# A hybrid encoder layer on one Trainium2 core: exponentials one tick behind their maxima, more gate buffers, gates spread up to the projections, softmax sums inverted behind their transpose

## The chip, the cores and the metric

One core of one Trainium2 chip runs the whole program as a single launch. Its engines run side by side, each in its own program order, and wait for one another by semaphores: TensorE (PE, matmuls and transposes; PEld is its weight load), VectorE (DVE), ScalarE (ACT), GpSimd (POOL) and SyncE (SP), which here only issues DMA transfers, all of them from one queue in program order. The metric is the device time of one execution in microseconds (us); lower is better.

## The reference

One layer on `x` of 1024 tokens by 1024 channels, float32. A first RMS norm and one combined projection give the inputs of two mixers and of two merge gates:

```python
proj = rmsnorm(x, attn_norm_g) @ w_in          # 1024 x 8096
c_q, c_kv, k_rope, z_mla, q_dil, k_dil, v_dil, z_dil, g_mla, g_dil = split(proj)
a_out = mla_attention(c_q, c_kv, k_rope, ...)  # 8 heads, dense softmax over 1024 keys
y_mla = (a_out * silu(z_mla)) @ w_o_mla
d_out = dilated_mixture(q_dil, k_dil, v_dil)   # 3 groups of 8 heads, windows of
...                                            # dilation 1, 4, 16, merged by their sums
y_dil = (d_out * silu(z_dil)) @ w_o_dil
merged = sigmoid(g_mla + b) * y_mla + sigmoid(g_dil + b) * y_dil
return rmsnorm(x + merged @ w_out, final_norm_g)
```

## The kernel before

Every float32 product is made of three matmuls (`mm3`, L142 to L146: high by high, high by low, low by high parts), so that each operand is first split in two: a cast on ACT (L150) and a subtraction on DVE or POOL (L151). A group of three matmuls of 512 columns is called a **step** here.

The program has five stretches. Up to about 220 us it makes latents, rotary tables and the dilated values; up to about 545 us the dilated queries and keys (`blocks`). Then comes **dilated attention** (to about 832 us), then **latent attention** (to about 1120 us), and last the projections and the output.

*Dilated attention* (`attention`, L1316) is software-pipelined over 72 units: four head pairs, each with 8 units of group 0, 8 of group 1 (`dil_head`, four units a head) and 2 of group 2 (`dil_classes`). The loop L1330 runs ticks t = -2 to 73. In tick t it transposes the probabilities of unit t on PE and copies them out on ACT (`do(t, 3)`, L1144 and L1152), scores unit t+2 on PE (L1120, L1121, or L1231), takes the low part of unit t's transposed probabilities on DVE (L1156), takes the maxima of unit t+2 on DVE (L1130), and later in the same tick the exponentials of unit t+2 on ACT (`do(t + 2, 2)`, L1137); values of unit t-1 follow on PE (L1168, L1175). When the last unit of a head or class group has been scored, the operands of the item after next are loaded into the buffers that this frees (L1339).

Between these the tick *feeds* PE twice with steps of other work (`feed`, L66, a credit counter): `DIL_FEED[g]` steps each time, where g is the group of unit t: 1.33 for groups 0 and 1, 2.3 for group 2. The work fed is `gate_fill` (L718): 16 weight tiles (8 of the z gates, then 8 of the merge gates) by two halves are 32 jobs of 8 steps, 256 steps in all. A job ends in a tail: DVE multiplies the bank by the tokens' factors into a gate buffer `zg_z` (L728), ACT makes a tanh (L730 or L734), POOL two products for z gates (L731, L732), and SP stores the result. Gate buffers are `zg_z` and `zg_t`, two each, in the 128x2048 tile `zt`. The next weight tile is loaded (`w_raw`) at a job's first step and split four steps on.

*Latent attention* (`mla_attention`, L1008) runs 128 ticks: 32 units k (a head and 256 queries) by 4 ticks c. Each tick transposes a quarter of unit k's probabilities (L871), copies them on ACT (L873), takes their low part on DVE (L879), and multiplies by the values of a tick before (L895, L896). Scores, maxima (L855) and exponentials (L863, their sums go to `m_den`) of unit k+1 run in ticks c = 0 to 2. Ticks c = 2 and 3 feed PE with `self.rate` steps. Gates that are left are spread over the ticks before `GATES_END` = 29; nothing is fed from then to `PROJ_BEGIN` = 33, where the dilated projection (`proj_fill`) takes over.

After the second head of a pair, each half of the tokens ends with a division by the softmax sums, eight times in all, at k = 5, 7, 13, 15, 21, 23, 27, 31. `mla_factors` (L917) doubles and inverts the sums on DVE as 128x8 in the last tick of the unit before; `mla_spread` (L929) transposes the result on PE to 8x128 (L938), copies it on ACT (L940), and SP sends it through DRAM (`s_mr`) to all partitions; `mla_gated` multiplies it by the gate on POOL (L953), `mla_weighted` applies it on DVE (L960), and `mla_merged` splits the result (L967). In tick 0 of a unit DVE's order is: low part, then the maxima of the next unit.

The order on each engine in both attention stretches is the order in which the code is written (a manual schedule).

## Time and profile before

| | us |
|---|---|
| median of the runs (two of the three at 1252.39 and 1254.29; one, 4276.14, is far off) | 1254.29 |
| the profiled execution's own time | 1254.46 |
| its span, first to last instruction | 1252.5 |
| TensorE busy in the span | 1212.4 (97%) |
| VectorE, ScalarE, GpSimd busy | 730.8, 622.0, 570.2 |
| mean granted TensorE clock | 0.990 |
| DMA share of the 16 engines, whole span | 59.5% |

All durations below come from that one execution. A busy TensorE is not TensorE at its peak: matmuls overlap, so that a matmul of 0.39 us can start 0.23 us after the one before it. What the engine can lose is its idle time, and stretches in which its granted clock is under 1. On the page, "<-" behind an idle time names what ended it.

### The profile page before, as it was taken

How to read it: one execution, taken by the hardware profiler on the slowest of the kernel's cores; microseconds unless marked ns; L12 is line 12 of the kernel's file. 1: busy time of each engine (PE TensorE's matmuls, PEld its weight loads, DVE VectorE, ACT ScalarE, POOL GpSimd, SP SyncE). 2: the span in 40 equal slices, each digit the busy share in tenths (PEclk: the TensorE clock that was granted, in tenths of full speed). 3: DMA queues.
4: the chain of work that ended last, by engine and by line, in shares of the span. 5: the costliest groups of instructions: out<-in, count | busy, mean ns of one | idle time of the engine just before them, and what ended most of it. 6: DMA issues, size and time to landing. Idle time of an engine off the chain costs nothing.

```text
span 1252.5 us, 19486 instructions
## 1 busy us (share of the span) xinstructions
PE 1212.4 (97%) x6909; PEld 1064.5 (85%) x6909; DVE 730.8 (58%) x1304; ACT 622.0 (50%) x1300; POOL 570.2 (46%) x482
## 2 busy tenths in 40 slices
PE   8979999999999999999999999999999999999998
PEld 8979999888888888888888889878878888888886
DVE  7473534467657653345555575647766767759542
ACT  6534345444343344455554666545655656654232
POOL 2352218877777777543464442415521201168322
PEclk9989999999999999999999999899999999999999
DMA  9847589365445642496887898964634445225241
GB/s 333 225 157 283 196 302 317 103 180 156 135 132 165 174 127 100 122 268 197 233 257 200 207 294 212 266 175 116 178 128 119 110 118 135 85 96 182 84 151 51
DMA packets 126416, 221.37 MB, mean 177 GB/s; under 512 B 28072, under 2 KB 60400, under 8 KB 121392
## 3 DMA queue, kind: packets, MB, share of 16 engines
q1 hardware_dynamic: 126320, 220.14, 59.5%
q8 instruction: 54, 0.88, 0.3%
q14 instruction: 42, 0.34, 0.1%
HBM read 149.24 MB, written 70.85 MB: 176 GB/s over the span
## 4 chain that ended last, share of the span: by engine, by line
PE 75%; DMA 11%; DVE 4%; ACT 4%; issue 3%; POOL 1%; SPq 1%; ACTq 0%; POOLq 0%; DVEq 0%
PE bank L145 5%; PE bank L144 5%; PE bank L146 5%; PE pj L145 4%; PE bank L871 4%; PE pj L144 4%; PE pj L146 4%; DMA at_r<-s_dk 3%; PE st_a L144 2%; PE st_a L145 2%; PE st_d L145 2%; PE st_c L145 2%; PE st_d L146 2%; PE st_a L146 2%; PE st_c L146 2%
## 5 line engine op out<-in xcount | busy, mean ns | idle before, releaser
L151 POOL TENSOR_TENSOR w_l<-w_raw,w_h 128x512 fp32r<-128x512 f32 x188 | 247.5, 1330 | 276.7 <-ACT w_h L150 218.1
L150 ACT CAST w_h<-w_raw 128x512 fp32r<-128x512 f32 x188 | 112.6, 621 | 110.1 <-POOL w_raw L495 92.7
L144 PE MATMUL bank<-at_r,w_h 128*128 128x512 f32 x344 | 142.8, 415 | 0.0
L879 DVE TENSOR_TENSOR at_r<-bank,at_r 128x512 fp32r<-128x512 f32 x128 | 88.0, 688 | 84.5 <-ACT at_r L873 84.2
L145 PE MATMUL bank<-at_r,w_h 128*128 128x512 f32 x344 | 136.6, 397 | 0.6 <-POOL at_r L151 0.6
L146 PE MATMUL bank<-at_r,w_l 128*128 128x512 f32 x344 | 136.7, 397 | 0.0
L873 ACT CAST at_r<-bank 128x512 fp32r<-128x512 f32 x128 | 74.9, 586 | 72.5 <-PE bank L871 71.9
L145 PE MATMUL pj<-w_l,at_r 128*128 128x256 f32 x384 | 109.7, 286 | 0.0
L146 PE MATMUL pj<-w_h,at_r 128*128 128x256 f32 x384 | 109.6, 285 | 0.0
L144 PE MATMUL pj<-w_h,at_r 128*128 128x256 f32 x384 | 109.5, 285 | 0.0
L1137 ACT ACTIVATE at_f<-at_f,at_f 128x256 f32<-128x256 f32 x128 | 64.1, 502 | 52.1 <-DVE at_f L1130 51.8
L1156 DVE TENSOR_TENSOR at_r<-bank,at_r 128x512 fp32r<-128x512 f32 x64 | 43.9, 686 | 70.4 <-ACT at_r L1152 70.3
L495 POOL TENSOR_TENSOR w_raw<-w_raw 128x512 f32<-128x512 f32 x64 | 82.8, 1294 | 0.1
L871 PE MATMUL bank<-consts,at_f 128*128 128x128 f32 x512 | 77.2, 273 | 1.7 <-ACT at_f L863 1.1
L146 PEld LDWEIGHTS bank<-at_r,w_l 128*128 128x128 f32 x344 | 65.7, 191 | 14.9
L146 PEld LDWEIGHTS pj<-w_h,at_r 128*128 128x128 f32 x384 | 74.2, 193 | 1.0
L145 PEld LDWEIGHTS pj<-w_l,at_r 128*128 128x128 f32 x384 | 74.3, 193 | 0.7
L144 PEld LDWEIGHTS pj<-w_h,at_r 128*128 128x128 f32 x384 | 74.2, 193 | 0.7
L145 PEld LDWEIGHTS bank<-at_r,w_h 128*128 128x128 f32 x344 | 65.9, 192 | 9.9 <-POOL at_r L151 1.0
L144 PEld LDWEIGHTS bank<-at_r,w_h 128*128 128x128 f32 x344 | 65.8, 191 | 9.2
L895 PE MATMUL bank<-at_r,at_r 128*128 128x256 f32 x256 | 67.7, 285 | 1.3 <-ACT at_r L873 1.3
L896 PE MATMUL bank<-at_r,at_r 128*128 128x256 f32 x256 | 67.5, 285 | 0.9 <-DVE at_r L879 0.9
(321 smaller groups left out, 3325.3 us busy)
## 6 DMA issues: line engine op xcount, KB each, us to landing
w_raw<-wt SPq DMA_DIRECT2D x48, 512.0 KB, 3.7
at_r<-s_dq SPq DMA_DIRECT2D x32, 512.0 KB, 7.3
s_dk<-dq_st SPq DMA_DIRECT2D x80, 128.0 KB, 2.4
s_dv<-dv_st SPq DMA_DIRECT2D x32, 256.0 KB, 3.0
s_dq<-dq_st SPq DMA_DIRECT2D x64, 128.0 KB, 2.4
zt<-s_gt SPq DMA_DIRECT2D x32, 256.0 KB, 4.5
w_raw<-wv SPq DMA_DIRECT2D x12, 512.0 KB, 5.8
at_r<-s_dk SPq DMA_DIRECT2D x8, 576.0 KB, 11.3
```

The costliest lines, as they stand in the source:

```text
L144: mm(out, lh, rh, start=start, stop=False, skip_group_check=skip)
L145: mm(out, lh, rl, start=False, stop=False, skip_group_check=skip)
L146: return mm(out, ll, rh, start=False, stop=stop, skip_group_check=skip)
L150: self.nc.scalar.copy(out=h, in_=raw)
L151: sub.tensor_tensor(out=l, in0=raw, in1=h.bitcast(F32), op=ALU.subtract)
L495: self.nc.gpsimd.tensor_tensor(out=b[out], in0=b[x], in1=b[y], op=ALU.subtract)
L871: self.nc.tensor.transpose(pt[:, o:o + 128], self.P[k, b][:, 128 * kc:128 * kc + 128], self.ident)
L873: self.nc.scalar.copy(out=h, in_=pt)
L879: self.nc.vector.tensor_tensor(out=l, in0=pt, in1=h.bitcast(F32), op=ALU.subtract)
L895: mm(out, vv[:, kc], ph[:, x], start=kc == 0, stop=False)
L896: mm(out, vv[:, kc], pl[:, x], start=False, stop=kc == 7)
L1137: nc.scalar.activation(out=p, in_=p, func=AF.Exp, scale=-1.0, bias=nm, accum_out=den)
```

## The change

- **Exponentials** of unit t+1, not t+2, run in tick t, and stand directly behind the maxima of unit t+2 and ahead of the feeds. So they come a tick after their maxima, and in the tick ahead of their transposes.
- **Feed**: 1.26 steps in place of 1.33 for groups 0 and 1, and the group is that of unit t+2, the one whose scores are made, not of unit t. At the end of dilated attention steps are fed up to 224 of 256, and the credit is cleared.
- **Gate buffers**: `zg_t` gets two more places, in the unused ends of the key buffers of the dilated heads; jobs 16 to 25 have four places (`zg_g`, all of `zt`) in place of two.
- **Gates to the projections**: `GATES_END` is 33, so that the 32 steps left are 2 in each of the 16 ticks before it that feed. The tokens' factors `R` stay in use longer; one operand of the dilated projection (`brd`, its last) is therefore cut in halves of which one lies where the masks were, and the masks get a fixed address. The two merges at k = 5 and 7 move one unit later, since their place is still read by the gates.
- **Softmax sums**: `mla_factors` is gone. `mla_spread` transposes the sums themselves, and DVE doubles and inverts them from PSUM as 8x128, ahead of the next maxima. ACT's copy is gone.

```diff
-DIL_FEED = (1.33, 1.33, 2.3, 1.8)
+DIL_FEED = (1.26, 1.26, 2.3, 1.8)
+WIDE_END = 26
-GATES_END, PROJ_BEGIN = 29, 33
+GATES_END = PROJ_BEGIN = 33
...
-        for name, k in (("zg_z", 0), ("zg_t", 2), ("br_x", 2), ("gate", 0)):
-            self.places[name] = [right[:, 512 * (k + i):512 * (k + i) + 512] for i in range(4 if name == "gate" else 2)]
+        x = [right[:, 512 * i:512 * i + 512] for i in range(4)]
+        self.places.update(zg_z=x[:2], zg_t=x[2:] + [22528, 30720], zg_g=x, br_x=x[2:], gate=x)
...
-            z = self.get("zg_z")
+            z = self.get("zg_g" if 16 <= job < WIDE_END else "zg_z")
...
-    def mla_factors(self, k):
...
-        d = self.md = self.ep.tile([128, 2, 4], F32, name="m_d", bufs=2)
-        v.tensor_scalar(out=d, in0=self.stats[pair][1][:, :, 4 * half:4 * half + 4], scalar1=2.0, scalar2=None, op0=ALU.mult)
-        v.reciprocal(out=d, in_=d)
...
-        nc.tensor.transpose(tp[:8, :128], d.rearrange("p h b -> p (h b)"), self.ident)
+        nc.tensor.transpose(tp[:8, :128], self.stats[pair][1][:, half].rearrange("p h b -> p (h b)"), self.ident)
         ds = self.get("av_t")[:8, :128]
-        nc.scalar.copy(out=ds, in_=tp[:8, :128])
+        nc.vector.tensor_scalar(out=ds, in0=tp[:8, :128], scalar1=2.0, scalar2=None, op0=ALU.mult)
+        nc.vector.reciprocal(out=ds, in_=ds)
...
-                for n in ((k - 1,) if k not in (6, 7) else (5,) if k == 7 else ()):
+                for n in {6: (), 7: (), 8: (5,), 9: (7,)}.get(k, (k - 1,)):
                     self.mla_merged(n, self.nc.gpsimd)
             else:
                 self.mla_gated(k)
-                self.mla_factors(k + 1)
...
         for t in range(-2, N + 2):
-            g = units[min(max(t, 0), N - 1)][0] if t <= N else 3
+            g = units[min(t + 2, N - 1)][0] if t <= N else 3
             do(t, 3)
             do(t + 2, 0)
             do(t, 4)
             do(t + 2, 1)
+            do(t + 1, 2)
...
             self.feed(DIL_FEED[g])
             do(t - 2, 6)
-            do(t + 2, 2)
             do(t - 2, 7)
...
+        while self.steps < len(ZG) * 16 - 32:
+            self.steps += 1
+            next(self.fill)
+        self.owed = 0.0
         self.mla_attention(later, N + 2)
...
-                            m = cp.tile([128, 896], F32, name="masks")
+                            cp.tile([128, 896], F32, name="masks")
+                            m = self.hand(2048, 896)
...
-            p = [self.shaped(92160 + 4096 * i, [128, S], F32R) for i in range(7)] + [self.hand(RIGHT, S, F32R)]
+            p = [self.shaped(92160 + 4096 * i, [128, S], F32R) for i in range(7)]
+            p = [(x[:, 0:512], x[:, 512:S]) for x in p] + [(self.hand(2048, 512, F32R), self.hand(RIGHT, 512, F32R))]
```

Three places show how instructions move. In the listings, a row is an instruction of the built program, `at_..._f` and `at_..._r` are buffers at fixed addresses, `bank`, `left` and `right` are PSUM. Line numbers of the changed kernel are 13 or so lower in attention.

ScalarE, where the first pair passes from group 0 (`at_2432_r`) to group 1 (`at_512_r`), before. L1152 copies transposed probabilities, L1137 are a unit's two exponentials, L730 a gate's tanh, L1180 copies the lower half of a head's values:

```order
L1152 CAST at_2432_r<-bank_5438 128x512
L1137 ACTIVATE at_512_f,at_96_f<-at_512_f,at_96_f 128x256 x2
L1152 CAST at_2432_r<-bank_5439 128x512
L730 ACTIVATE zt<-zt 128x512
L1180 COPY at_512_f<-left_5445 64x512
L1137 ACTIVATE at_512_f,at_96_f<-at_512_f,at_96_f 128x256 x2
L1152 CAST at_512_r<-bank_5438 128x512
```

The same place in the changed kernel, with L1139, L1124, L731 and L1167 for the four:

```order
L1139 CAST at_2432_r<-bank_5441 128x512
L1124 ACTIVATE at_512_f,at_96_f<-at_512_f,at_96_f 128x256 x2
L1139 CAST at_2432_r<-bank_5442 128x512
L1124 ACTIVATE at_512_f,at_96_f<-at_512_f,at_96_f 128x256 x2
L1167 COPY at_512_f<-left_5448 64x512
L731 ACTIVATE at_512_f<-zt 128x512
L1139 CAST at_512_r<-bank_5441 128x512
```

The exponentials now follow the copy at once; the tanh and the copy of values, which stood ahead of them, stand behind them, and the tanh writes one of the new places.

SyncE's queue where the second head pair passes to the third, before. `s_dq`, `s_dk` and `s_dv` are the dilated queries, keys and values in DRAM, `wt` is a gate's weight tile, `s_rr` the merge's shares:

```order
L140 DMA w_raw<-wt 128x1024
L140 DMA at_512_f<-s_rr 64x512 x2
L140 DMA s_zs<-zt 128x512
L140 DMA at_2048_f<-s_dv_70 64x2048 x2
L140 DMA at_2048_r<-s_dq_62 64x2048 x2
L140 DMA at_1152_r<-s_dk_65 128x1152
```

The same place in the changed kernel:

```order
L141 DMA at_512_f<-s_rr 64x512 x2
L141 DMA at_2048_f<-s_dv_70 64x2048 x2
L141 DMA at_2048_r<-s_dq_62 64x2048 x2
L141 DMA at_1152_r<-s_dk_65 128x1152
L141 DMA w_raw<-wt 128x1024
```

The weight tile and a gate's store, which stood ahead of the first head of the third pair, stand behind it. At the passage to the second pair the tile already stands behind the keys; at the passage to the fourth it stays ahead of the values.

VectorE in latent attention around the first division, before (L926 and L927 are the doubling and the inversion, L879 low parts, L855 maxima, L1450 and L728 work of the merge and of a gate):

```order
L1450 TENSOR_TENSOR at_1024_f<-at_1024_f,at_512_f 128x512
L879 TENSOR_TENSOR at_512_r<-bank_5439,at_512_r 128x512
L728 TENSOR_TENSOR zt<-bank_5440,at_1024_f 128x512
L926 TENSOR_SCALAR m_d<-m_den 128x8
L927 RECIPROCAL m_d<-m_d 128x8
L879 TENSOR_TENSOR at_512_r<-bank_5438,at_512_r 128x512
L855 TENSOR_REDUCE m_nm<-right_8182 128x1
```

The same place in the changed kernel:

```order
L1441 TENSOR_TENSOR at_1024_f<-at_1024_f,at_512_f 128x512
L879 TENSOR_TENSOR at_512_r<-bank_5442,at_512_r 128x512
L879 TENSOR_TENSOR at_512_r<-bank_5441,at_512_r 128x512
L927 TENSOR_SCALAR at_512_f<-bank_5442 8x128
L928 RECIPROCAL at_512_f<-at_512_f 8x128
L855 TENSOR_REDUCE m_nm<-right_8169 128x1
```

Doubling and inversion move behind the low part of the next unit's first tick, read a bank of PSUM, and stand directly ahead of the maxima.

More of the change, by code (lines that the diff above doesn't have):

```diff
@@ L720, in gate_fill, with after @@
         nc = self.nc
-        def after(i, half, ps):
-            z = self.get("zg_z")
+        def after(job, i, half, ps):
+            z = self.get("zg_g" if 16 <= job < WIDE_END else "zg_z")
             t = self.get("zg_t") if i < 8 else z
@@ L760, in gate_fill @@
                 run_all(tail)
-                tail = after(i, half, ps)
+                tail = after(2 * n + half, i, half, ps)
                 if self.one_bank:
@@ L797, in proj_fill @@
             t = coming.pop(0)
-            br = self.brd if i else self.brm
+            br = self.brd if i else [[(x[:, 0:512], x[:, 512:S]) for x in y] for y in self.brm]
             for m, j in enumerate((0, 1, 3, 2) if i else range(4)):
                 x = dt % 2 * 4 + j if i else dt % 2 * 3 + j if j < 3 else 6 + dt % 2
-                self.mm3(ps, *self.at(w, x), br[0][j][:, c], br[1][j][:, c], m == 0, m == 3)
+                self.mm3(ps, *self.at(w, x), br[0][j][half], br[1][j][half], m == 0, m == 3)
                 if k == 0:
@@ L839, in mla_scores @@
         if (h, u, b) in ((h & 6, 0, 0),):
-            self.stats[h // 2] = [self.ep.tile([128, 2, 8], F32, name=f"m_{x}", bufs=2) for x in ("nm", "den")]
+            self.stats[h // 2] = [self.ep.tile([128, 2, 2, 4], F32, name=f"m_{x}", bufs=2) for x in ("nm", "den")]
         q, kk, _ = self.heads[h]
@@ L1030, in parts @@
             def parts():
[L1031 removed]
+                self.split(o["y"], self.brd[0][j][half], self.brd[1][j][half], nc.gpsimd)
             put(t, load)
@@ L1591, in run @@
             cp.tile([128, 16], F32, name="edge_c")
+            for c in "yu":
+                cp.tile([128, 1], F32, name=f"rh_{c}", bufs=2)
             self.cp = cp
```

15 lines of the change are left out of this document (3 added, 12 removed).

## Prediction

> **What bounds the kernel now.** I read three views in this order: the busy time of each engine by stretch, what TensorE waited for, and the timeline around its longest waits. First the stretches (columns: busy time and instruction count of each engine, granted TensorE clock, share and rate of the DMA engines):
>
> ```profile
> core 0: us, PE busy (x) PEld busy (x) DVE busy (x) ACT busy (x) POOL busy (x), PEclk, DMA share, GB/s
> 545.00:832.00 287.00, 276.87 (x1710) 245.30 (x1709) 167.99 (x425) 161.28 (x418) 124.18 (x122) 0.98 0.84 230
> 832.00:1095.00 263.00, 257.85 (x1567) 226.49 (x1566) 183.13 (x238) 159.18 (x287) 66.05 (x59) 0.99 0.46 126
> ```
>
> TensorE bounds every stretch that the change touches. Dilated attention leaves it idle for 287.00 - 276.87 = 10.1 us, latent attention for 263.00 - 257.85 = 5.2 us. The matmuls, transposes and their shapes stay the same, so the change can win only such idle time, and time at a lowered clock. The first 545 us keep their order. In dilated attention the DMA engines are 84% busy, which matters below.
>
> What TensorE waited for (us in total, times, longest), first in dilated attention, then behind it:
>
> ```profile
> PE right L1120 <- DMA at_r<-s_dk: 5.9, 3, 2.6
> PE bank L1144 <- ACT at_f L1137: 1.7, 8, 0.4
> PE left L1175 <- DVE at_r L1156: 1.6, 2, 1.3
> PE left L1175 <- ACT at_r L1152: 0.4, 1, 0.4
> PE left L1168 <- DVE at_r L1156: 0.3, 1, 0.3
> ...
> PE bank L938 <- DVE m_d L927: 2.1, 2, 1.2
> PE bank L895 <- ACT at_r L873: 1.3, 1, 1.3
> PE bank L896 <- DVE at_r L879: 0.9, 3, 0.3
> ```
>
> Two things stand out. The largest wait is not for an engine but for keys, three times, at the first scores of a new head pair. The next, 1.7 + 1.6 + 0.4 + 0.3 = 4.0 us, comes from ScalarE and VectorE being late with probabilities. Here is the first wait for keys with what follows it, and the other two:
>
> ```profile
> 597.17 0.60 PE L1248 MATMUL bank<-consts,at_f 128*128 128x128 f32 x4
> 599.16 0.39 PE L1120 MATMUL right<-at_r,at_r 128*128 128x256 f32 x1 [1.39 <-DMA at_r<-s_dk]
> ...
> 599.51 0.29 PE L1120 MATMUL right<-at_r,at_r 128*128 128x256 f32 x1
> 599.63 0.28 PE L1121 MATMUL right<-at_r,at_r 128*128 128x256 f32 x1
> 599.75 0.40 PE L144 MATMUL bank<-at_r,w_h 128*128 128x512 f32 x1
> 599.98 0.40 PE L145 MATMUL bank<-at_r,w_h 128*128 128x512 f32 x1
> 600.21 0.39 PE L146 MATMUL bank<-at_r,w_l 128*128 128x512 f32 x1
> ...
> 670.50 0.36 PE L1120 MATMUL right<-at_r,at_r 128*128 128x256 f32 x1 [1.92 <-DMA at_r<-s_dk]
> 743.68 0.36 PE L1120 MATMUL right<-at_r,at_r 128*128 128x256 f32 x1 [2.62 <-DMA at_r<-s_dk]
> ```
>
> Starts are 0.23 us apart at 512 columns and 0.12 at 256, so a step of three costs TensorE 0.69 us. The gate work fed stands right *behind* these waits: the tick whose scores wait asks for 2 x 2.3 steps only afterwards.
>
> The clock is a second loss. Four short windows, the columns as above:
>
> ```profile
> 670.00:675.00 5.00, 4.50 (x15) 3.68 (x16) 0.78 (x4) 1.09 (x4) 0.00 (x0) 0.66 1.00 232
> 744.00:750.00 6.00, 6.00 (x36) 5.24 (x35) 2.83 (x11) 3.93 (x10) 1.81 (x2) 1.00 1.02 240
> 805.00:811.00 6.00, 6.00 (x20) 5.13 (x20) 3.71 (x7) 2.05 (x6) 1.32 (x2) 0.50 1.01 199
> 920.00:924.00 4.00, 4.00 (x18) 3.44 (x17) 2.94 (x5) 2.45 (x5) 1.28 (x1) 0.57 0.64 215
> ```
>
> Behind the wait that ended at 670.50 the clock fell to 0.66, which loses 5.00 x 0.34 = 1.7 us; likewise 6.00 x 0.50 = 3.0 and 4.00 x 0.43 = 1.7 behind waits near 801 and 918. Behind the longest wait, 743.68, it did not fall.
>
> **The change, part by part.** The sum is made against the profiled execution, 1254.46 us, which is 0.17 above the median of the runs, 1254.29.
>
> *Feed by the group of unit t+2.* The keys of a new pair are asked for in the tick that scores the last unit of group 1, and needed three ticks later. The two ticks between score the classes; they were fed 2 x 1.33 = 2.66 steps each, now 2 x 2.3 = 4.60. With 0.14 less in the asking tick that is 2 x 1.94 - 0.14 = 3.74 steps, or 3.74 x 0.69 = 2.6 us more work ahead of the waiting scores. Waits of 1.39, 1.92 and 2.62 would vanish. But the transfers are slow for a reason:
>
> ```profile
> at_r<-s_dk SPq DMA_DIRECT2D x6, 576.0 KB, 12.0
> ```
>
> 12.0 us for 576 KB, beside queries, values, weights and stores, at a share of 1.0 in the windows above. The changed queue puts a weight tile behind the keys at the second passage (not at the third), which helps. The ticks after lose the same steps, so the next head's keys have 4 ticks at the lower feed. I take 5.0 of 5.9; ends 2.0 and 5.9.
>
> *Exponentials a tick later, more gate buffers.* ScalarE now waits neither for maxima of its own tick nor, with four places, for stores of gates. The rows of dilated attention (idle before and its releaser at the end):
>
> ```profile
> L1137 ACT ACTIVATE at_f<-at_f,at_f 128x256 f32<-128x256 f32 x124 | 62.1, 502 | 51.1 <-DVE at_f L1130 50.8
> L1152 ACT CAST at_r<-bank 128x512 fp32r<-128x512 f32 x63 | 36.5, 579 | 14.6 <-PE bank L1144 13.6
> L1180 ACT COPY at_f<-left 64x512 f32<-64x512 f32 x32 | 18.7, 583 | 0.7
> L150 ACT CAST w_h<-w_raw 128x512 fp32r<-128x512 f32 x26 | 14.7, 616 | 0.0
> L730 ACT ACTIVATE zt<-zt 128x512 f32<-128x512 f32 x15 | 9.4, 629 | 18.7 <-DVE zt L728 12.5 <-DMA s_zs<-zt 6.2
> ```
>
> The 50.8 us are the old order's price on ScalarE; TensorE felt 4.0 us of it. I take back 3.0, since VectorE's own waits for the merge stay; ends 0 and 4.0. With the waits go most of the clock dips behind them, 1.7 + 3.0 = 4.7 us: I take 3.0, ends 0 and 4.7.
>
> The price: a unit's exponentials now end just ahead of its transposes, where they had a tick to spare. From one tick's transposes to the next, ScalarE's path is 0.60 (four transposes) + 0.58 (copy) + 2 x 0.50 = 2.2 us. TensorE's shortest tick, one without values, is about 0.45 (four transposes to the next start) + 4 x 0.12 + 2 x 0.69 = 2.3 us. Only 0.1 us is spare, less what semaphores take. Weight casts (2 x 0.62), a tanh (0.63) and the copy of values (0.58) come behind the exponentials and push the next copy back; the next tick, with ten value matmuls of 0.12, absorbs 1.2. Not in the trace is how often they meet: 26 casts are 13 pairs. Ends 0 and 13 x 0.3 = 4; I take 2.0 lost.
>
> *Fewer steps.* Counting the credits, the old loop feeds 229 steps by the end of dilated attention, the new one 224: 5 x 0.69 = 3.5 us move into latent attention. Nothing is lost or won on a full TensorE: 0.
>
> *Gates up to tick 33.* Old ticks 30 and 31 fed nothing, while the second division of the first pair ran its chain through DRAM. ScalarE's first work behind it:
>
> ```profile
> 917.44 0.62 ACT L150 CAST at_r<-zt 128x512 fp32r<-128x512 f32 x1 [3.79 <-POOL zt L1028]
> ```
>
> There TensorE waited for low parts (2 x 0.34 of the 0.9) and for a copy (1.3) which stood on ScalarE behind this cast, and the cast waited 3.79 for GpSimd, which stood behind the chain; then the clock fell (1.7). Now 4 steps, 2.8 us of matmuls, lie in these ticks: 2.0 + 1.7 = 3.7 can go, I take 3.0; ends 1.0 and 3.7. SyncE waits for the last gate's store before it loads the second gate of the projections; that one is used a unit later, so 0. The merges moved by one unit are needed only by the last projections: 0. Masks and the cut operand change addresses alone: 0.
>
> *Sums inverted behind their transpose.* The rows:
>
> ```profile
> L926 DVE TENSOR_SCALAR m_d<-m_den 128x8 f32<-128x8 f32 x8 | 4.4, 550 | 0.0
> L927 DVE RECIPROCAL m_d<-m_d 128x8 f32<-128x8 f32 x8 | 1.6, 203 | 0.3
> L1426 DVE RECIPROCAL at_f<-at_f 16x128 f32<-16x128 f32 x1 | 0.9, 930 | 0.0
> ...
> ACT at_f L940 <- PE bank L938: 12.7, 8, 2.4
> ```
>
> The transposes no longer wait for VectorE: the 2.1 us go (ends 1.0 and 2.4, since a wait of 0.28 follows each). But inversion gets dearer: its time follows the elements per partition, 8 in 0.20 us, 128 in 0.93. With a doubling of some 0.25 (the shortest rows of 128x8 are 0.16) VectorE's part is 1.2 us where it was 0.75. And it now waits for the transpose, as ScalarE's copy did (12.7 / 8 = 1.6 us each, the last row); with the low part of 0.69 done meanwhile, 0.9. Behind it stand the maxima of the next unit, then exponentials and low parts: some 2.1 us late, eight times. VectorE idles 30% of this stretch (183.13 of 263.00), about 11 us per division, so it catches up within the unit. I take 0.5 lost; ends 0 and 2.0.
>
> The sum: -5.0 - 3.0 - 3.0 + 2.0 - 3.0 - 2.1 + 0.5 = -13.6, so 1254.46 - 13.6 = 1240.9, say **1241 us**. All good ends give -20.7 (1234), all bad ones +2.0 (1256).
>
> **The rivals.**
>
> *Transfers stay the limit* (1247 us). The same bytes move in less time at a share of 0.84, so keys land later by what TensorE has gained. Then of 5.9 only 1.0 comes back, and of the dips 1.3: 1241 + 4.0 + 1.7 = 1246.7. For it: the 12.0 us and shares of 1.0. Against it: 2.6 us of cover do not depend on the share.
>
> *The clock dips are not caused by these waits* (1246 us). Three waits, of 1.92, 1.30 and 1.30 us, had a dip behind them, one of 2.62 and one of 1.39 had none. If dips come by chance, none of the 3.0 comes back, nor 1.7 of the 3.0 at tick 31: 1241 + 4.7 = 1245.7.
> The Trainium skill, page "TensorE: Matmul & The Clock Gate", section "What's actually happening", says that the clock halves after at least one idle window of about 3.4 us; by that rule waits this short cost no clock, and the time is that of this rival. The trace does not agree on the length, since all three dips follow waits under 2 us.
>
> *Exponentials become the bound* (slower, 1260 us). If the path of 2.2 us is longer than TensorE's tick by 0.3 us on average, through semaphores or casts, 72 ticks lose 21.6 us, against gains of 15.6 without the 2.0 counted: 1254.46 - 15.6 + 21.6 = 1260.5. It decides from 15.6 / 72 = 0.22 us a tick. For it: only 0.1 is spare in the shortest ticks. Against it: most ticks have 0.5 to 1.9 us more on TensorE.
>
> *The change moves waits without removing them* (1252 us): with the phases of gates and merges shifted, other meetings of VectorE's and GpSimd's long rows replace those of before; only the 2.1 us of L938 are sure.
>
> **How the numbers follow.** 0.50 for the forecast, 0.24 for the transfers, 0.13 for the clock, 0.08 for the exponentials, 0.05 for the last. The range is 1232 to 1255: the good ends, with 2 us for short waits that a matmul's modelled end hides, up to the bad ends; it leaves out most of the slower rival and little else. 2% is 25 us, about what a measurement of this kernel can tell from no change. Faster by that means 1229, more than all idle and clock counted: 0.04. Slower by that needs (25 + 15.6) / 72 = 0.56 us a tick: 0.04. Within: 0.92.
>
> **What would show it.** Right: no wait of L1120's successor for keys above 0.5 us; the idle of the exponentials for maxima down from 50.8 to a few us; dilated attention shorter by 8 to 14 us, of which 3.5 only move; a granted clock of 1.00 there; no wait of the sums' transposes, and the reciprocals at 0.9 us. Wrong: transposes waiting for exponentials in most ticks (third rival), keys still waited for (first), or low parts of latent attention late behind the eight reciprocals.

## The result and the profile after

| | before | after |
|---|---|---|
| median of the runs beside each other, us | 1253.93 | 1244.02 |
| the profiled execution's own time | 1254.46 | 1242.97 |
| its span | 1252.5 | 1240.9 |
| mean granted TensorE clock | 0.990 | 0.997 |

The ratio is 0.9931, with a 95% interval of 0.9909 to 0.9953: faster by 0.7%, clear of no change, and within the 2% that the forecast named. (One of the four runs before, 4276.14, is far off; it is in the median, which is 1253.57 without it, but not in the ratio, which is made of fast runs alone.) The forecast was 1241 us with a range of 1232 to 1255: the profiled execution is 2.0 us above it, the median 3.0. The sum was nearly right, but its two halves, dilated and latent attention, were not. To see it, both profiled executions are cut at the same events: the first transposes of dilated attention, the first of latent attention, and the first of latent attention's tick 40. First before, the two stretches in which something changed (length, busy time and count of PE, PEld, DVE, ACT, POOL, granted clock, share and rate of the DMA engines):

```profile
542.20:836.50 294.30, 283.34 (x1743) 250.45 (x1741) 171.90 (x430) 163.83 (x422) 126.08 (x125) 0.98 0.84 231
836.50:933.00 96.50, 92.17 (x545) 79.68 (x544) 64.17 (x84) 59.41 (x107) 44.24 (x42) 0.98 0.53 148
```

The same two after, and the two behind them (the third was 155.30 before, too, the last 164.20):

```profile
542.30:818.80 276.50, 272.71 (x1727) 243.65 (x1726) 170.58 (x429) 161.07 (x425) 125.65 (x125) 1.00 0.87 243
818.80:922.40 103.60, 95.47 (x560) 82.09 (x559) 64.17 (x85) 59.73 (x106) 43.76 (x42) 0.98 0.52 146
922.40:1077.70 155.30, 155.30 (x968) 138.33 (x967) 112.46 (x144) 92.29 (x165) 20.43 (x16) 1.00 0.40 106
1077.70:1240.90 163.20, 155.76 (x771) 131.09 (x768) 92.38 (x142) 61.74 (x127) 71.43 (x51) 1.00 0.35 118
```

Dilated attention is 17.8 us shorter, of which 3.5 are the five steps that moved out of it; 14.3 are won. TensorE's idle time there fell from 294.30 - 283.34 = 11.0 us to 276.50 - 272.71 = 3.8, and the clock is 1.00. Latent attention's first 40 ticks are 7.1 us *longer*. The five steps explain 3.5 (TensorE's busy time rose by 95.47 - 92.17 = 3.3); the other 3.6 is idle time, 8.1 us where it had been 4.3 (not all of this is the change's, see below). The 72 ticks behind them have no idle time in either kernel, and the last stretch is 1.0 shorter. In all -17.8 + 7.1 + 0.1 - 1.0 = -11.6, the difference of the spans.

What TensorE waited for after (us in total, times, longest), first in dilated attention, then in the 40 ticks:

```profile
PE bank L1131 <- ACT at_f L1124: 2.2, 4, 1.5
PE left L145 <- DVE at_f L1255: 0.8, 1, 0.8
PE right L1107 <- DMA at_r<-s_dk: 0.8, 1, 0.8
```

```profile
PE bank L895 <- DVE at_f L911: 3.3, 3, 2.0
PE bank L895 <- ACT at_r L873: 2.9, 1, 2.9
PE bank L871 <- ACT at_f L863: 1.1, 1, 1.1
```

The keys (L1107) went from 5.9 us to 0.8, and transposes now wait a little for exponentials (L1131, 2.2). In latent attention the values wait 3.3 us for the sums of the accumulators (L911) and 2.9 for a copy (L873), where before there was one wait for a copy, of 1.3; the wait for doubled sums is gone. The row of dilated attention's exponentials, over the whole span, shows that the change did what it says on ScalarE (busy, mean ns | idle before, releaser):

```profile
L1124 ACT ACTIVATE at_f<-at_f,at_f 128x256 f32<-128x256 f32 x128 | 64.1, 504 | 3.0 <-DVE at_f L1117 3.0
```

The idle time of 51 us ahead of the exponentials is 3.0 now. TensorE had felt 4.0 of the 51, so this drop by itself says nothing of the time.

### Where the 40 ticks lost it

Three places in the changed kernel's timeline (start, length, engine, line, operands, in brackets the idle time before and what ended it). The first, GpSimd, ScalarE, VectorE and TensorE near 842 us:

```profile
836.92 2.54 POOL L152 TENSOR_TENSOR w_l<-w_raw,w_h 128x512 fp32r<-128x512 f32 x2
839.42 1.28 POOL L1015 TENSOR_TENSOR zt<-zt,at_f 128x512 f32<-128x512 f32 x1
840.73 0.62 ACT L151 CAST at_r<-zt 128x512 fp32r<-128x512 f32 x1 [3.35 <-POOL zt L1015]
841.86 0.58 ACT L902 COPY at_f<-bank 64x512 f32<-64x512 f32 x1
843.61 0.67 DVE L911 TENSOR_TENSOR at_f<-bank,at_f 64x512 f32<-64x512 f32 x1
844.33 0.38 PE L895 MATMUL bank<-at_r,at_r 128*128 128x256 f32 x1 [1.97 <-DVE at_f L911]
```

A piece is one of the eight parts (a head pair, half the tokens) of the dilated projection's operand: GpSimd multiplies it by its gate (L1015), and a tick later ScalarE casts the product (L151). The split of a gate's weight tile (L152, 2.54 us for its two rows) now stands just ahead of that product. So ScalarE waits 3.35 us at the cast, the copies behind it in its queue come late, VectorE's sum too, and TensorE 1.97.

The second, near 862 us:

```profile
861.00 0.69 DVE L729 TENSOR_TENSOR zt<-bank,at_f 128x512 f32<-128x512 f32 x1 [2.58 <-DMA s_gt<-zt]
863.33 0.67 DVE L911 TENSOR_TENSOR at_f<-bank,at_f 64x512 f32<-64x512 f32 x1
864.06 0.39 PE L895 MATMUL bank<-at_r,at_r 128*128 128x256 f32 x1 [1.05 <-DVE at_f L911]
```

A gate's eviction waits 2.58 us for the store of the gate before the last: jobs from 26 on have two places, and the jobs left now run on to tick 33. The third is the meeting near the second division, which the change was to fill with matmuls:

```profile
891.83 0.94 DVE L928 RECIPROCAL at_f<-at_f 8x128 f32<-8x128 f32 x1
893.16 0.29 SPq L141 DMA_DIRECT2D s_mr<-at_f  x1
900.39 1.09 SPq L141 DMA_DIRECT2D at_f<-s_mr  x2
903.90 1.29 POOL L941 TENSOR_TENSOR at_f<-at_f 128x512 f32<-128x512 f32 x1 [5.20 <-DMA at_f<-s_mr]
905.15 1.26 POOL L1015 TENSOR_TENSOR zt<-zt,at_f 128x512 f32<-128x512 f32 x1
906.45 0.62 ACT L151 CAST at_r<-zt 128x512 fp32r<-128x512 f32 x1 [5.08 <-POOL zt L1015]
908.35 0.42 PE L895 MATMUL bank<-at_r,at_r 128*128 128x256 f32 x1 [2.92 <-ACT at_r L873]
```

And before, from the copy of the inverted sums to the product with the gate:

```profile
905.64 0.25 ACT L940 COPY at_f<-bank 8x128 f32<-8x128 f32 x1 [1.39 <-PE bank L938]
905.92 0.29 SPq L140 DMA_DIRECT2D s_mr<-at_f  x1
914.87 1.28 POOL L953 TENSOR_TENSOR at_f<-at_f 128x512 f32<-128x512 f32 x1 [1.63 <-DMA at_f<-s_mr]
```

From the transposed sums to the product with the gate it was 914.87 - 905.64 = 9.2 us; now, from the doubling at 891.52, it is 12.4. Of the 3.2 us more, the inversion (0.94 and the 0.28 of the doubling, where a copy of 0.25 stood) is about 1, the start of the write behind it 0.4, and the way through memory, from the issue of the write to the product, the rest: 10.7 us in place of 9.0. The 4 steps, 2.8 us of matmuls, that were to fill the hole went in, and the hole grew by as much. The wait is 2.92 us (1.3 before), and the clock fell behind it as it had before.

The longer way through memory is not shown to come from the change. Two kernels that are described below, the exponentials alone and the gate buffers alone, have the steps and the code of these 40 ticks as before, and the same transfers ahead of the write. The way took 10.7 and 10.5 us there, and TensorE waited 3.0 and 2.9 us for the same copy. The first of the two:

```profile
PE bank L895 <- ACT at_r L873: 3.0, 1, 3.0
```

In all, TensorE was idle for 6.0 and 5.9 us in their 40 ticks. So the execution before, with 9.0, 1.3 and 4.3, had a short way, and about 1.6 of the 3.8 us that the changed kernel is idle more may be of this kind. What the way consists of can be guessed from all 14 profiled executions. Where the write was issued 6.5 to 7.7 us behind the first load of the next head's queries and keys, the read followed after another 5.1 to 8.1; in the two kernels with the pieces earlier (below) it was issued 11.5 and 12.4 us behind, and the read followed after 1.7 and 1.2. That fits a write that lands only once the loads ahead of it on the queue have landed; it was not tested by itself.

### The profile page after: what moved, and what is told of

The parts are those of the page before. It is cut to its first block, busy times and chain, and to the rows that moved or that the text cites. A ratio compares the mean times of both kernels' runs of the same rounds, so it can differ in the third digit from the quotient of the medians.

```text
span 1240.9 us, 19482 instructions
## 1 busy us (share of the span) xinstructions
PE 1206.6 (97%) x6909; PEld 1060.0 (85%) x6909; DVE 729.7 (59%) x1304; ACT 616.0 (50%) x1292; POOL 568.8 (46%) x482
## 4 chain that ended last, share of the span: by engine, by line
PE 71%; DMA 9%; POOL 4%; issue 2%; ACT 2%; DVE 2%; SPq 1%; ACTq 0%; POOLq 0%; DVEq 0%
PE bank L145 6%; PE bank L146 6%; PE bank L147 6%; PE bank L871 3%; PE st_a L145 2%; PE st_a L147 2%; PE st_a L146 2%; PE st_d L145 2%; PE st_c L145 2%; PE st_d L147 2%; PE st_c L147 2%; PE st_c L146 2%; PE st_d L146 2%; PE bank L896 2%; PE right L145 2%
## 5 line engine op out<-in xcount | busy, mean ns | idle before, releaser
L152 POOL TENSOR_TENSOR w_l<-w_raw,w_h 128x512 fp32r<-128x512 f32 x188 | 246.1, 1322 | 231.0 <-ACT w_h L151 180.8
L151 ACT CAST w_h<-w_raw 128x512 fp32r<-128x512 f32 x188 | 112.1, 621 | 106.5 <-POOL w_raw L496 90.7
L145 PE MATMUL bank<-at_r,w_h 128*128 128x512 f32 x344 | 141.7, 412 | 0.0
L879 DVE TENSOR_TENSOR at_r<-bank,at_r 128x512 fp32r<-128x512 f32 x128 | 88.0, 688 | 82.6 <-ACT at_r L873 82.2
L146 PE MATMUL bank<-at_r,w_h 128*128 128x512 f32 x344 | 134.9, 392 | 0.6 <-POOL at_r L152 0.6
L873 ACT CAST at_r<-bank 128x512 fp32r<-128x512 f32 x128 | 74.9, 586 | 75.5 <-PE bank L871 74.8
L1124 ACT ACTIVATE at_f<-at_f,at_f 128x256 f32<-128x256 f32 x128 | 64.1, 504 | 3.0 <-DVE at_f L1117 3.0
```

Of the source, the lines that this page charges most:

```text
L145: mm(out, lh, rh, start=start, stop=False, skip_group_check=skip)
L146: mm(out, lh, rl, start=False, stop=False, skip_group_check=skip)
L151: self.nc.scalar.copy(out=h, in_=raw)
L152: sub.tensor_tensor(out=l, in0=raw, in1=h.bitcast(F32), op=ALU.subtract)
L873: self.nc.scalar.copy(out=h, in_=pt)
L879: self.nc.vector.tensor_tensor(out=l, in0=pt, in1=h.bitcast(F32), op=ALU.subtract)
```

## The experiments

All times are medians; a ratio is against runs of the kernel before on the same chip. Beside the four kernels with one run, one run of the kernel before took 1255.1. The stretches are those of the profiled execution; "clock" is the time in it that granted clocks under 1 took away, counted as if TensorE had been busy (a fall that overlaps a wait costs less).

| kernel | us | ratio, 95% interval | dilated attention, clock | first 40 latent ticks, clock |
|---|---|---|---|---|
| before | 1253.9 | | 294.3, 5.1 | 96.5, 1.7 |
| after | 1244.0 | 0.9931, 0.9909 to 0.9953 | 276.5, 0 | 103.6, 1.7 |
| dilated part | 1245.5 | 0.9936, 0.9913 to 0.9959 | 277.6, 0 | 105.2, 1.7 |
| latent part | 1249.7 | 0.9977, 0.9950 to 1.0004 | 298.0, 6.8 | 99.0, 1.7 |
| feed alone | 1248.2 | one run | 279.9, 3.4 | 107.2, 5.1 |
| exponentials alone | 1258.7 | one run | 297.5, 8.5 | 96.6, 0 |
| gate buffers alone | 1256.4 | one run | 298.1, 8.5 | 98.0, 1.7 |
| after, old feed | 1253.4 | one run | 294.3, 6.8 | 98.6, 1.7 |
| after, gates to tick 29 | 1244.5 | 0.9931, 0.9900 to 0.9961 | 274.7, 0 | 108.6, 5.1 |
| after, old sums | 1241.4 | 0.9916, 0.9884 to 0.9948 | 274.6, 0 | 106.3, 5.1 |
| after, splits later | 1237.6 | 0.9873, 0.9852 to 0.9893 | 278.5, 3.4 | 98.8, 0 |
| after, pieces earlier | 1242.5 | 0.9915, 0.9890 to 0.9941 | 274.9, 0 | 102.9, 3.4 |
| the same, more places | 1238.7 | 0.9896, 0.9849 to 0.9943 | 274.6, 0 | 100.9, 3.4 |
| after, three settings | 1236.4 | 0.9859, 0.9827 to 0.9891 | 280.2, 1.7 | 98.3, 1.7 |

The first 540 us, the same instructions in every kernel, took 538.4 to 543.4 us in these executions, which alone moves a time by as much. So single runs are read by stretches.

**The dilated part alone.** The kernel before with the feed, the exponentials, the buffers and the steps fed up to 224; latent attention as it was:

```diff
...
+        while self.steps < len(ZG) * 16 - 32:
+            self.steps += 1
+            next(self.fill)
+        self.owed = 0.0
         self.mla_attention(later, N + 2)
```

> The kernel before with the parts of the change in dilated attention alone (feed by the group of unit t+2, exponentials a tick later, gate buffers, 224 steps at its end); gates end at tick 29, sums are inverted as before. Theory (the whole gain is made in dilated attention, and the change in latent attention gives part of it back): first transposes of latent attention at 819 us as in the changed kernel (836 before); latent attention and the rest take 416 + 3 us instead of 422, so about 1240 to 1242 us, below the changed kernel's 1244. Rival (the latent part is worth the 4.6 us that were forecast for it, and the loss there comes from the dilated part's new phases): 1244 to 1249.

Measured: 1245.5 us, above the theory's range and in the rival's. Dilated attention has nearly the whole gain (277.6). The 40 ticks took 105.2, longer than in the changed kernel, though no line of latent attention differs from before. Its longest wait there:

```profile
PE bank L145 <- DVE zt L729: 4.5, 2, 3.6
```

A gate's step waits 3.6 us for an eviction, and this eviction, at 860.07 us, had waited 3.79 for a store of a gate. So the loss in latent attention does not need the latent edits: TensorE is idle for 9.4 us in these ticks, and for 9.2 with the feed alone. It comes with the five steps more and the phase at which the gates enter the stretch; which of the two was not tested. The rival's other half, that the latent edits are worth 4.6 us, is for the next kernel.

**The latent part alone.** The changed kernel with feed, exponentials and gate buffers as before, and without the steps up to 224:

```diff
-DIL_FEED = (1.26, 1.26, 2.3, 1.8)
+DIL_FEED = (1.33, 1.33, 2.3, 1.8)
...
-        self.places.update(zg_z=x[:2], zg_t=x[2:] + [22528, 30720], zg_g=x, br_x=x[2:], gate=x)
+        self.places.update(zg_z=x[:2], zg_t=x[2:], zg_g=x[:2], br_x=x[2:], gate=x)
...
-            g = units[min(t + 2, N - 1)][0] if t <= N else 3
+            g = units[min(max(t, 0), N - 1)][0] if t <= N else 3
...
-            do(t + 1, 2)
...
+            do(t + 2, 2)
...
-        while self.steps < len(ZG) * 16 - 32:
-            self.steps += 1
-            next(self.fill)
-        self.owed = 0.0
```

> The kernel before with the parts in latent attention alone (gates to tick 33, merges a unit later, sums inverted behind their transpose); feed, exponentials and gate buffers in dilated attention as before. Theory: dilated attention stays at 836 us for the first transposes; the latent part is worth -2 us (sums) against waits of some 3 us at tick 34: 1252 to 1257 us, no gain. Rival (the latent part is worth the 4.6 us forecast): 1249 to 1250.

Measured: 1249.7 us, the ten runs between 1245.3 and 1261.5, which can't be told from no change, though the median is as the rival has it (1249 to 1250). The profiled execution is the slowest of them, so only its stretches count: the 40 ticks took 99.0 where they had been 96.5, with no step moved into them, and the last stretch 163.2 in place of 164.2. A wait for a copy of 3.2 us stands in these ticks:

```profile
PE bank L895 <- ACT at_r L873: 3.2, 1, 3.2
```

The gates up to tick 33 filled nothing here that can be seen. Of the latent edits, only the sums show a gain, some 1 us at the end, and that one is steady: from tick 112 on, the eight profiled executions with the new order take 163.2 or 163.3 us, the six with the old one 164.2 to 165.8.

**The feed alone, the exponentials alone, the buffers alone, and all but the feed.** Four kernels, each run once, for what they show of dilated attention.

The feed alone, on the kernel before:

```diff
-DIL_FEED = (1.33, 1.33, 2.3, 1.8)
+DIL_FEED = (1.26, 1.26, 2.3, 1.8)
...
-            g = units[min(max(t, 0), N - 1)][0] if t <= N else 3
+            g = units[min(t + 2, N - 1)][0] if t <= N else 3
```

The exponentials alone, on the kernel before:

```diff
+            do(t + 1, 2)
...
-            do(t + 2, 2)
```

The gate buffers alone, on the kernel before:

```diff
+        self.places.update(zg_z=x[:2], zg_t=x[2:] + [22528, 30720], zg_g=x, br_x=x[2:], gate=x)
...
+            z = self.get("zg_g" if 16 <= job < WIDE_END else "zg_z")
```

All but the feed: the changed kernel with the first of these edits undone.

> The kernel before with the feed alone changed (1.26 steps, and the group of unit t+2). By the end of dilated attention 224 steps are fed, not 229, which alone moves 3.5 us behind it. Theory (the extra steps stand ahead of the scores that wait for keys, and cover the transfer): waits for keys fall from 5.9 to under 1 us in all, the clock dip behind the second one goes, and latent attention begins at 825 to 828 us (836 before). Rival (transfers are the limit, keys come later): waits of 4 us or more, 831 to 833.

> The kernel before with the exponentials alone moved a tick later. Theory (ScalarE no longer stands behind VectorE's maxima, and two-place gate buffers still hold both up): ScalarE's idle time for maxima falls from 50.8 to under 8 us, but of the 4.0 us that TensorE waits in dilated attention only half goes; waits for keys stay at 5 to 6 us; latent attention begins at 832 to 835 us. Rival (exponentials now too near their transposes): transposes wait 5 us or more for exponentials, 838 to 842.

> The kernel before with more gate buffers alone. Theory: waits of ScalarE for s_zs (6.2 us) and of VectorE for s_gt in dilated attention go, and with them TensorE's waits near 656 us (2.1) and 801 us (2.4, and the dip of 3.0 behind it); latent attention begins at 829 to 834 us. Rival (VectorE waits for the merge anyway): 835 to 837.

> The changed kernel with the feed as before (1.33 steps, group of unit t), so 229 steps by the end of dilated attention. Theory: three waits for keys of together 5 us or more are back, with a dip or two (1.7 us each); latent attention begins at 819 + 3.5 + 5 to 9 = 827 to 831 us. Rival (the exponentials and buffers alone removed the waits): 822 to 824.

Measured: dilated attention of 279.9, 297.5, 298.1 and 294.3 us, where it was 294.3 before and 276.5 after. With the feed alone latent attention begins at 819.6 us, earlier than expected; for the exponentials alone and the buffers alone it begins where the rivals had it (839.1 and 836.5), and for all but the feed later than either range (834.4). TensorE's waits there with the feed alone:

```profile
PE bank L1144 <- ACT at_f L1137: 2.4, 4, 1.7
PE left L144 <- DVE at_f L1268: 0.8, 1, 0.8
PE right L1120 <- DMA at_r<-s_dk: 0.4, 1, 0.4
```

With the exponentials alone:

```profile
PE bank L1144 <- ACT at_f L1137: 6.9, 5, 3.9
PE right L1120 <- DMA at_r<-s_dk: 3.1, 2, 1.9
PE left L1175 <- DVE at_r L1156: 1.8, 1, 1.8
```

With the gate buffers alone, and with all but the feed:

```profile
PE right L1121 <- DMA at_r<-s_dk: 7.6, 3, 3.6
```

```profile
PE bank L1131 <- ACT at_f L1124: 4.4, 6, 2.1
PE right L1107 <- DMA at_r<-s_dk: 3.0, 2, 1.9
PE bank L145 <- DVE zt L729: 2.0, 1, 2.0
```

The feed is what won. TensorE's idle time in dilated attention was 11.0 us before; it is 3.7 with the feed alone, 12.7 with the exponentials alone, 12.4 with the buffers alone, 10.8 with all but the feed, and 3.8 after. Over all 14 profiled executions it is 2.1 to 5.5 us in the nine with the new feed, and 10.8 to 13.0 in the five with the old one. The feed alone takes the keys from 5.9 us to 0.4, and the waits for VectorE's low parts with them; what is left, 3.6 us, is about what the full change has too, and the 3.4 us between 279.9 and 276.5 are one fall of the clock behind a wait of 1.7. ScalarE's idle time for maxima is still 47.7 us with the feed alone: TensorE's idle time went without it, and stayed where the exponentials' new order took it away. Without the feed, the exponentials put waits of 6.9 or 4.4 us ahead of the transposes, more than the 4.0 they were to remove, and half the keys' wait is left. With the old feed the 40 latent ticks, too, are nearer to those of before (98.6), although all latent edits are in: TensorE is idle for 6.2 us there, as in the two kernels with none of these edits (6.0 and 5.9). So most of the loss there goes with the feed. That the feed also makes the late exponentials harmless fits its place: it puts two more steps on TensorE in the ticks that score classes.

**Gates only to tick 29.**

```diff
-GATES_END = PROJ_BEGIN = 33
+GATES_END, PROJ_BEGIN = 29, 33
```

> The changed kernel with gates ending at tick 29 again, so 2.29 steps in each of 14 ticks and none in ticks 30 and 31. Theory (the wait at tick 34 is for the sums' chain through DRAM, whose length does not depend on the gates): the chain is issued into fewer steps of work, so TensorE waits longer at ticks 30 to 34, by up to the 2.8 us of work taken out; the total stays within 1 us of the changed kernel's 1244, since the same steps stand elsewhere. Rival (gates in ticks 28 to 33 load the queue and so lengthen the chain): shorter, by 3 us or more.

Measured: 1244.5 us, the same ratio as the changed kernel. Without the clock the 40 ticks took 108.6 - 5.1 = 103.5 us, against 103.6 - 1.7 = 101.9. The waits are others and as long:

```profile
PE bank L145 <- DVE zt L729: 3.3, 2, 2.2
PE bank L895 <- ACT at_r L873: 2.7, 1, 2.7
PE bank L895 <- DVE at_f L911: 2.0, 1, 2.0
```

The wait for the copy, 2.7 us, stands with empty ticks as with filled ones. In the total, the gates up to tick 33 are worth nothing that can be measured.

**The splits of three pieces later.** Those of the first two pieces two ticks later, that of the last four. In this kernel the last piece's buffer has by then been loaded with a gate of the projections, so that this piece's operand is the gate; the work is the same.

```diff
-            put(t + gap + 1, parts)
+            put(t + gap + (3 if t < 3 else 5 if t == 26 else 1), parts)
```

> The changed kernel with the two casts that held ScalarE up moved later: the halves of the first two pieces are split two ticks later, those of the last piece four ticks later. Theory (ScalarE stands behind a cast that waits for GpSimd, which stands behind a weight split or behind the sums' chain): the waits of TensorE at 842 (2.1 us) and 905 us (2.9 us and the short ones and the dip behind it, about 2 more) go, those for a gate's store (1.2 us at 862) stay: 4 to 7 us below the changed kernel, 1237 to 1240. Rival (GpSimd or the chain itself is late, and the wait moves to the next that needs it): within 1.5 us of 1244.

Measured: 1237.6 us, 6.4 under the changed kernel's, and the intervals do not meet. The 40 ticks took 98.8, 4.8 less, of which 1.7 are the clock. The waits near 842 and 905 us, 1.97 and 2.92, are gone, but for 0.6 and 0.2 at the second; the one near 862 stays and is 2.3 in place of 1.05. TensorE's idle time fell from 8.1 to 5.0. So the two were real costs of these queues, and not a sign of work that TensorE had to do anyway. The way through memory still took 11.0 us at the second division: what cost TensorE was the cast that stood ahead of the copy on ScalarE and waited for the end of that way.

**Pieces earlier, and more places.** The products of the second and third pairs' pieces a tick earlier, the first two splits two ticks later; the second kernel has four places besides for the gates of jobs 28 to 31. In both, the piece loaded at tick 17 takes the buffer that holds shares of the last pair until tick 18, so that half a class of the dilated mixture is weighted with a gate.

```diff
-PIECES = (1, 0, 0), (2, 0, 1), (14, 3, 0), (16, 3, 1), (18, 1, 0), (20, 1, 1), (24, 2, 0), (26, 2, 1)
+PIECES = (1, 0, 0), (2, 0, 1), (14, 3, 0), (16, 3, 1), (17, 1, 0), (19, 1, 1), (23, 2, 0), (25, 2, 1)
...
-            put(t + gap + 1, parts)
+            put(t + gap + (3 if t < 3 else 1), parts)
```

The second kernel besides (`zg_y` has four places of its own):

```diff
-            z = self.get("zg_g" if 16 <= job < WIDE_END else "zg_z")
+            z = self.get("zg_g" if 16 <= job < WIDE_END else "zg_z" if job < 28 else "zg_y")
```

> The changed kernel with the piece products of the second and third head pairs one tick earlier (17, 19, 23, 25) and the weight splits of the first two pieces two ticks later, so that no split stands ahead of a piece product on GpSimd. Theory (in latent attention's first 40 ticks the changed kernel pays for meetings of GpSimd's splits with the piece products): TensorE's wait for the copied sums near 842 us and the wait near 905 us for a cast queued behind the piece product go; the first 40 ticks take about 99 us in place of 103.6, and the time is 1237 to 1240. Rival (the waits are only moved: VectorE's and GpSimd's long rows meet at other places): 1242 to 1245, with new waits of 3 us or more at those engines' rows in the same stretch.

> The kernel with the pieces moved, and besides four places of their own for the gates of jobs 28 to 31, in place of the two that they share. Theory: VectorE's gate eviction near 862 us no longer waits for the store of an earlier gate (2.6 us on the changed kernel), so TensorE's wait for VectorE's sums there goes (1.0 to 2 us), and the time is 1 to 2.5 us under that of the kernel with the pieces moved: 1235 to 1238.5. Rival: the two are equal within 0.5 us, since the wait there has another cause.

Measured: 1242.5 and 1238.7 us. The first misses: its rival holds. The waits near 842 and 905 went, but two for VectorE's sums are longer. TensorE's row, and VectorE's own behind one of them:

```profile
PE bank L895 <- DVE at_f L911: 6.1, 2, 3.7
```

```profile
DVE zt L729 <- DMA s_gt<-zt: 4.0, 1, 4.0
```

One, 2.43 us, is the kind near 862: an eviction now waits 4.0 us for a store. With more places both rows are gone, and of TensorE's 6.1 us 3.7 are left. That is the other wait, which both kernels have; it is a meeting as near 842, with a weight tile's split, and then the low part of another piece, ahead of the earlier piece's product. In the kernel with more places:

```profile
871.54 2.54 POOL L152 TENSOR_TENSOR w_l<-w_raw,w_h 128x512 fp32r<-128x512 f32 x2 [1.54 <-ACT w_h L151]
876.60 0.62 ACT L151 CAST at_r<-zt 128x512 fp32r<-128x512 f32 x1 [3.61 <-POOL zt L1015]
880.33 0.58 PE L895 MATMUL bank<-at_r,at_r 128*128 128x256 f32 x1 [3.75 <-DVE at_f L911]
```

(The buffer that two uses share makes VectorE wait too, 3.0 and 4.2 us, but TensorE waits for nothing behind that.) So the places do what was expected of them. In the total, 3.8 us, it can't be shown from these two, whose intervals overlap widely; 1238.67 is just above the range expected.

**The old sums in the changed kernel.** Doubling and inversion ahead of the transpose, ScalarE's copy behind it.

```diff
-        nc.vector.tensor_scalar(out=ds, in0=tp[:8, :128], scalar1=2.0, scalar2=None, op0=ALU.mult)
-        nc.vector.reciprocal(out=ds, in_=ds)
+        nc.scalar.copy(out=ds, in_=tp[:8, :128])
...
+                self.mla_factors(k + 1)
```

> The changed kernel with the old inversion: the sums are doubled and inverted on VectorE ahead of their transpose, and ScalarE copies the transposed result. Theory (the new inversion gains what the prediction took, 2.1 - 0.5): TensorE's waits for the doubled sums come back at 1 to 2.5 us in all, and the time is 1245 to 1247. Rival (VectorE's longer part ahead of the maxima costs as much as the waits gained): 1242.5 to 1244.5, with the waits back but less idle of the exponentials for maxima in latent attention.

Measured: 1241.4 us, below both ranges; the interval of its ratio overlaps that of the changed kernel over most of its length. Of the waits for the doubled sums one came back, 1.2 us, and the last stretch is 164.5 in place of 163.2. In the 40 ticks the meeting at the second division is still there, longer:

```profile
PE bank L895 <- ACT at_r L873: 4.1, 1, 4.1
```

So the theory falls as far as the total goes: the new order wins about a microsecond in the last stretch, and no more can be shown.

**Three settings.** The first two splits two ticks later; the last piece's product and split one tick earlier, ahead of the product with the inverted sums in GpSimd's queue; four places for the gates of jobs 28 to 31.

```diff
-        self.places.update(zg_z=x[:2], zg_t=x[2:] + [22528, 30720], zg_g=x, br_x=x[2:], gate=x)
+        self.places.update(zg_z=x[:2], zg_t=x[2:] + [22528, 30720], zg_g=x, zg_y=[36864, 45056, 38912, 47104], br_x=x[2:], gate=x)
...
-            z = self.get("zg_g" if 16 <= job < WIDE_END else "zg_z")
+            z = self.get("zg_g" if 16 <= job < WIDE_END else "zg_z" if job < 28 else "zg_y")
...
+            gap -= t == 26
             put(t + gap, product)
-            put(t + gap + 1, parts)
+            put(t + gap + (3 if t < 3 else 1), parts)
```

> The changed kernel with three settings of latent attention's first 40 ticks: the splits of the first two pieces two ticks later (9 and 10 in place of 7 and 8), the product and split of the last piece one tick earlier (30 and 31), ahead of the multiplication by the inverted sums in GpSimd's queue, and four places of their own for the gates of jobs 28 to 31. All else is the changed kernel's. Theory (the 3 to 4 us that these ticks lose are queues of GpSimd and ScalarE standing behind the piece products and the division's chain, and an eviction standing behind a store): TensorE's waits near 842, 862 and 905 us go, the 40 ticks take 97 to 100 us in place of 103.6, and the time is 1236 to 1240. Rival (the meetings only move, as they did with the second and third pairs' pieces a tick earlier): a wait of 3 us or more at another division or piece, and 1241 to 1244.

Measured: 1236.4 us, ratio 0.9859 (0.9827 to 0.9891): faster than before and than the changed kernel, whose interval lies above it. The 40 ticks, in a profiled execution that was one of its two slowest:

```profile
822.00:920.30 98.30, 94.27 (x559) 82.26 (x558) 64.89 (x84) 59.73 (x106) 43.91 (x42) 0.98 0.53 153
```

The waits near 842 and 862 are gone. The third is not: it is 2.42 us, with another head. GpSimd's product no longer stands behind the chain of the sums; it waits for the load of its piece:

```profile
899.56 1.28 POOL L1015 TENSOR_TENSOR zt<-zt,at_f 128x512 f32<-128x512 f32 x1 [1.26 <-DMA zt<-s_da]
900.87 0.62 ACT L151 CAST at_r<-zt 128x512 fp32r<-128x512 f32 x1 [3.45 <-POOL zt L1015]
904.60 0.58 PE L895 MATMUL bank<-at_r,at_r 128*128 128x256 f32 x1 [2.42 <-DVE at_f L911]
```

A load issued 1.3 us earlier might cure this one. That was not tried.

## Why the prediction was right, and where it was not

*What bounds the kernel: right.* TensorE bounds every stretch, and what was won is its idle time and its clock.

*Keys, -5.0: right in size and cause.* 5.9 us became 0.8 (the sign that it named, none above 0.5, was just missed), and only the kernels with the new feed have it. The transfers did not stay the limit: that rival needed the keys to land later by what TensorE gained, and with the feed alone 0.4 us of wait was left. It is not always gone, though: in the execution with the three settings, the keys were waited for once for 2.9.

*Exponentials and gate buffers, -3.0, and their price, +2.0: the net was right, the cause wrong.* Forecast -1.0 net; the waits for probabilities went from 4.0 to 2.2, the price within its bounds. But the feed alone comes to 2.4, with ScalarE still waiting 47.7 us for maxima. What the prediction called the gain of the exponentials' new order is a gain of the feed, and the order alone left TensorE idle for 12.7 us in place of 11.0. The step that failed is the reading that a wait on ScalarE's row, 50.8 us for maxima, causes the waits on TensorE's.

*Clock, -3.0: -5.1.* None was lost in dilated attention after. Over all eight executions with this dilated part it was 0 in six, and 1.7 and 3.4 in the others, 0.6 on average; so the forecast was too small, and the 0 is the usual case. (One of its windows was also cut short: the dip near 805 took 3.4, not 3.0.) The rival that dips are not caused by waits is refuted below; its number, 1246, is nearer to the median than the forecast all the same.

*Hidden in busy rows: not in the sum.* Keys, probabilities and clock make 5.1 + 1.8 + 5.1 = 12.0 of the 14.3. The other 2.3 are in rows of matmuls that stand as busy: busy time fell by 10.6, of which 3.5 moved and 5.1 were at half clock. The prediction had 2 us of this in its range, not in its sum.

*Fewer steps, 0: right.* 3.3 us more busy time in the 40 ticks.

*Gates up to tick 33, -3.0: failed.* The hole at the second division was to be covered by 4 steps. The step that failed is the length of the chain, taken as fixed: it was 3.2 us longer, 1.4 by the sums' own new order and 1.8 by the way through memory, which took 8.8 to 10.7 us in kernels whose code there had not changed. The wait of 1.3 that the prediction read was a short one. And two more meetings came, near 842 and 862. With the gates ending at tick 29 the time is the same. The prediction counted the five steps as moved at no price; the dilated part alone shows that they and the new phase cost waits where no line was changed. For this stretch the last rival, which it gave 0.05, was the right one: waits moved, and here grew. It was wrong for dilated attention, where they went.

*Sums, -2.1 and +0.5: too large.* The reciprocal took 0.94 us, where 0.93 were worked out, the doubling 0.28. About 1 us shows, in the last stretch; in the first 40 ticks, where the sums' chain ends later, nothing does.

So -9.0 for dilated attention was -14.3, and -4.6 for latent attention was +3.6 - 1.0 = +2.6. The forecast of 1241 was met by two errors of opposite sign, 5.3 and 7.2 us, so that the total came so near was luck. Dilated attention also became shorter by 17.8 us in all, beyond the 8 to 14 that were to show that it was right.

## What to carry to other kernels

A wait of the bounding engine is removed by putting work ahead of it on that engine, as the feed did here; taking idle time from another engine does nothing until the bounding engine is seen to wait for it. A gain in one stretch shifts the phase of all that follows, so look at the next stretch for long rows (here 2.5 us of a weight split) that may come to stand ahead of short rows with someone behind them, and price that with both signs. A hole filled with work is only filled if the chain that makes it stays as long, and a wait read from one execution can be a short one. Taking the row that waits for the chain out from ahead of the others in its queue was worth more here: with the splits later TensorE's wait for that copy fell to 0.2 us, though the way through memory took 11.0.

## What the hardware showed unasked

TensorE's clock falls in portions. Two stretches of the runs, the first with the exponentials alone, the second with all but the feed (columns as in the windows above):

```profile
655.00:663.00 8.00, 6.76 (x24) 5.61 (x25) 4.59 (x12) 4.82 (x14) 6.96 (x6) 0.57 1.01 248
```

```profile
824.00:832.00 8.00, 8.00 (x29) 6.56 (x29) 3.21 (x4) 1.83 (x4) 0.00 (x0) 0.57 0.34 104
```

8.00 x 0.43 = 3.4 us lost, in each. In all 14 profiled executions every fall except the one at the kernel's end lasted 3.4 us or two or three times that, at half clock, so that it took away 1.7, 3.4 or 5.1 us of full clock, and every one began within 3.4 us of an idle time of TensorE of 1.2 us or more. The idle times by their length, and those with a fall behind them (the 5.5 to 6.1 us at each kernel's start, ahead of the first clock record, are left out): under 1.2 us (from 0.7), 0 of 55; 1.2 to 1.5, 5 of 21; 1.5 to 2.0, 11 of 23; 2.0 to 2.5, 12 of 21; 2.5 to 3.4, 11 of 15; above, 13 of 13. So a wait from 1.2 to 3.4 us costs, beside itself, up to 1.0 us on average (39 falls after 80 such waits, 82 us in all). Whether a given one is followed by a fall can't be told beforehand from these records; shorter ones were followed by none. The three dips that the prediction ascribed to waits are of this kind; that the long wait of 2.62 us had none was luck.

The Trainium skill, page "TensorE: Matmul & The Clock Gate", section "What's actually happening", says that the clock is 4/8 after at least one idle window of about 3.4 us, in windows that run freely and do not start with the kernel. The length of the portions agrees; that the engine must be idle for a whole window does not, with 39 falls behind waits shorter than that.
